# Two-layer decoder trunk on one Trainium2 core: the dilated attention stage gets a written-out order on TensorE, with scores three blocks ahead and value products of four blocks together

## The chip, the cores and the metric

The kernel runs on one core of a Trainium2 chip. The metric is device microseconds of one execution; three runs of the kernel before lie between 3378.36 and 3381.26 us. The core has five engines that work side by side, each on its own list of instructions in order: TensorE (PE in the profile, its weight loads PEld), VectorE (DVE), ScalarE (ACT), GpSimd (POOL) and SyncE (SP), which here only issues transfers. An instruction that waits holds up everything behind it on its engine, and nothing on another engine.

## The reference

Two layers; each normalises x, projects it, mixes tokens in two branches and projects back. The branch that matters here is causal attention of 12 heads of width 64 over 2048 tokens, in three patterns, whose outputs are weighted by their softmax denominators:

```python
DIL_PATTERNS = ((128, 1), (512, 4), (2048, 16))     # window, dilation
def _dilated_window(q, k, v, window, dilation):      # blocks of 128 queries of one residue class
    ...                                              # each sees its own block of keys and the one before
    s = einsum('brnqhd,brnkhd->brnhqk', qb, kk) * scale;  s = where(mask, s, -inf)
    m = max(s, -1);  p = exp(s - m);  l = sum(p, -1)
    o = einsum('brnhqk,brnkhd->brnqhd', p, vv) / l
    return o, m + log(l)
def _dilated_mixture(q, k, v):
    alpha = softmax(stack(dens, 0), 0)               # over the three patterns
    return sum(alpha[..., None] * outs, 0)
```

## The kernel before, in words

A layer is four stages: input projection, the stick-breaking branch (`_stick`), the dilated branch (`_dilated`) and the output projection. `_dilated` goes over 6 pairs of heads, for each pair over the three patterns p = 0, 1, 2, and for each pattern over 16 blocks b of 128 queries: 288 blocks in a layer. A block's work:

- **scores** on TensorE: for each of the two heads two matmuls, the high and low part of the keys (lines 758 and 759), 256 columns each;
- **minimum and mask** on VectorE, one per head (line 760), then **exp** on ScalarE (line 764). They are 128 columns wide for p = 0 and for blocks with no predecessor, and 256 otherwise;
- **transposes** of the exps on TensorE (line 772), two or four, and a copy of them out of PSUM (line 774), on VectorE or ScalarE;
- **value products** on TensorE (line 779), two or four; the trace shows each as two records. Every fourth block the sums are copied to `o3` by ScalarE (lines 785, 788, 792).

When a pair is through, `stats` turns the minima and sums into weights `wr` (some small matmuls, lines 667 to 672, and a chain of small operations), and `apply` spreads the weights by one matmul for each of 16 columns (`weighing`, line 703), multiplies `o3` by them on VectorE (line 706), and adds and gates the three patterns on POOL (lines 710 to 712). Both run during the next pair. For the last pair the weighing lies between the output projection's matmuls, in threes (lines 841, 844, 845). `make_q` reorders the queries for p = 1 and p = 2 by casts, nearly all on POOL (lines 607, 612).

**Array shapes.** The profile writes the shape in which a matmul uses the 128 x 128 array: scores, transposes and the output projection 128\*128, value products 128\*64 (64 output rows for each head), weighing 64\*128 (contraction over 64 partitions), statistics 128\*32.

**What sets the order.** A scheduler that knows the program, not the chip, orders the instructions that are not pinned. In `_stick` TensorE's instructions are pinned in the order in which they are written; in `_dilated` only the last pair's weighing and a few of the first casts are.

Of the kernel before, what the change touches and what calls it, by code (L numbers as in the profile page):

```python
# [29 lines left out]
def _constants():  # L30
# [20 lines left out]
    sel = np.zeros((64, 16, 128), f)  # L51
# [509 lines left out]
def _dilated(tc, mem, v_scr, qk_scr, g_scr, mix, masks, sel, ident, neg1):  # L561
    nc = tc.nc
    mk = mem.get("M", [128, 732])
# [8 lines left out]
    ts_s = Slices([ta[:, 0], ta[:, 1], tb[:, 0:512].rearrange("p (c h q) -> p c h q", c=2, h=2)])  # L572
# [4 lines left out]
    v_r = mem.ring("H2", "H3", "H4", "H5")  # L577
    selr = mem.get("F13", [64, NT, 128], F32R)
# [20 lines left out]
    def make_q(pr, p):  # L599
        eng = nc.vector if pr == 0 and p == 1 and 1 else nc.gpsimd  # L600
        for h in range(2):
# [3 lines left out]
            if p == 1:  # L605
                for c in range(4):
                    eng.tensor_copy(
                        tr[:, 512 * c:512 * c + 512].rearrange("p (n r a) -> p n r a", n=4, r=4),
                        qc[:, c::4].rearrange("p r (n a) -> p n r a", n=4))
            else:  # L610
                for c in range(4):
                    ins = nc.gpsimd.tensor_copy(
                        tr.rearrange("p (j c a) -> p j c a", j=NT, c=NT)[:, 4 * c:4 * c + 4],
                        qc[:, :, 32 * c:32 * c + 32].rearrange("p c (j a) -> p j c a", a=8))
                    if pr == 0:
                        tc.keep_in_program_order(ins)
# [11 lines left out]
    VAHEAD = 2  # L628
# [3 lines left out]
    for i in range(VAHEAD):  # L632
        load_v(i)

    fin = []

    def hooks(pr, p, b):
        if b % 8 == 0:
            load_v((pr * 3 + p) * 2 + b // 8 + VAHEAD)
        while fin and fin[0][0] <= 16 * p + b:  # L640
            fin.pop(0)[1]()
        if (p, b) == (0, 2):
            make_q(pr, 2)
        if pr + 1 < NPAIR:
            if (p, b) == (1, 0):
                load_k(pr + 1)
            if (p, b) == (1, 8):
                load_q(pr + 1)
            if (p, b) == (2, 4):
                make_q(pr + 1, 1)  # L650

    def stats(pr, st, wrs):
        sm = xa[0:32, 0:768].rearrange("p (s q a) -> p s q a", s=2, q=3)
        x4 = xa[:, 768:1024].rearrange("p (s n h r c) -> p s n h r c", s=2, n=4, h=2, r=4)
        x1 = gt_r.get([128, 2, 2 * NT, 8])
        nc.vector.tensor_tensor(
            out=x1, in0=st[:, :, 2].rearrange("p s h j -> p s (h j)").unsqueeze(3).to_broadcast([128, 2, 2 * NT, 8]),
            in1=mk[:, 692:700].unsqueeze(1).unsqueeze(1).to_broadcast([128, 2, 2 * NT, 8]), op=ALU.mult)
        for s in range(2):
            for h in range(2):  # L660
                nc.vector.tensor_tensor(
                    out=x4[:, s, :, h],
                    in0=st[:, s, 1, h].rearrange("p (c n) -> p n c", n=4).unsqueeze(2).to_broadcast([128, 4, 4, 4]),
                    in1=mk[:, 688:692].unsqueeze(1).unsqueeze(3).to_broadcast([128, 4, 4, 4]), op=ALU.mult)
        for s in range(2):
            ps = w_r.get([128, 512])
            nc.tensor.transpose(ps[:32, 0:128], st[:, s, 0].rearrange("p h b -> p (h b)"), ident)
            for n in range(4):
                nc.tensor.matmul(ps[:32, 128 + 32 * n:160 + 32 * n], x4[:, s, n].rearrange("p h r c -> p (h r c)"),
                                 mk[:, 700:732], start=True, stop=True)  # L670
            for h in range(2):
                nc.tensor.matmul(ps[:32, 256:384], mk[:, 656 - 16 * h:688 - 16 * h],
                                 x1[:, s, NT * h:NT * h + NT].rearrange("p j a -> p (j a)"),
                                 start=h == 0, stop=h == 1)
            nc.any.tensor_copy(sm[:, s].rearrange("p q a -> p (q a)"), ps[:32, :384])
# [19 lines left out]
    def apply(pr, o3, wrs, c4, m7=None):  # L695
# [5 lines left out]
        for c in range(4 * c4, 4 * c4 + 4):  # L701
            wb = w_r.get([128, 3, 128])
            ins = nc.tensor.matmul(wb, selr[:, c], wrs[0], start=True, stop=True)  # L703
            if final:
                tc.keep_in_program_order(ins)
# [185 lines left out]
```

## Time and profile before

| | us |
|---|---|
| median of three runs | 3379.39 |
| the profiled execution | 3379.84 |
| its span | 3378.1 |
| dilated stage, first layer (from 1027.2 to 1502.7) | 475.50 |
| of it TensorE busy | 474.81 |
| dilated stage, second layer (from 2707.5 to 3183) | 475.50 |
| of it TensorE busy | 474.56 |

The span is what the trace covers, 1.7 us less than the execution's own time. The mean granted TensorE clock is 0.998 of full speed. "Busy" runs from an instruction's start to its modelled end; TensorE's instructions overlap, so that the distance from one start to the next says more than the length of one.

### The profile page before, as it was taken

To read this page: it belongs to the slowest core of one execution; us is meant where nothing else is said; L and a number is where in the kernel's file an instruction comes from. 1 tells how busy PE (TensorE), PEld (TensorE's weight loads), DVE (VectorE), ACT (ScalarE), POOL (GpSimd) and SP (SyncE) were. 2 spreads that over 40 slices of the span, in tenths; PEclk is the share of its full clock that TensorE was granted. 3 is DMA by queue.
4 is the path that set the end of the run, shared out by engine and by line. 5 is a ranking of instruction groups with operands and counts; after the bars stand their busy time and mean duration, and the time that the engine had idled before them with its cause. 6 is when DMAs were issued, how large, how long until landed. Compare 5 with 4: busy or idle time off the path is not lost.

```text
span 3378.1 us, 67384 instructions
## 1 busy us (share of the span) xinstructions
PE 3326.0 (98%) x25808; PEld 2873.5 (85%) x25808; DVE 1735.1 (51%) x4279; ACT 1524.4 (45%) x4347; POOL 1233.6 (37%) x1200
## 2 busy tenths in 40 slices
PE   8999999999999999999999999999999999999999
PEld 8999999887777777777899999998877777777777
DVE  5034330117997777774240344301179977877721
ACT  5123321116777777761031233201167787777600
POOL 3067761104672332252021777511046722223500
PEclk9999999999999999999999999999999999999999
DMA  5122245316213555344341222452252145553443
GB/s 187 66 88 101 101 145 174 104 60 172 54 56 101 157 152 155 105 156 140 125 133 66 84 105 105 151 166 92 73 158 67 45 121 157 147 150 95 131 141 103
DMA packets 305922, 395.85 MB, mean 117 GB/s; under 512 B 16832, under 2 KB 225728, under 8 KB 295360
## 3 DMA queue, kind: packets, MB, share of 16 engines
q1 hardware_dynamic: 305600, 391.54, 37.5%
q8 instruction: 204, 3.34, 0.4%
q14 instruction: 118, 0.97, 0.1%
HBM read 234.19 MB, written 148.90 MB: 113 GB/s over the span
## 4 chain that ended last, share of the span: by engine, by line
PE 90%; DVE 3%; issue 3%; ACT 2%; POOL 2%; DMA 1%; SPq 0%; POOLq 0%; DVEq 0%; ACTq 0%
PE b L290 11%; PE b L291 11%; PE b L289 11%; PE b L779 8%; PE b L772 8%; PE b L758 5%; PE b L759 4%; PE b L841 4%; PE b L315 4%; PE b L317 3%; PE b L316 3%; PE b L844 3%; PE b L845 3%; PE b L528 3%; PE b L703 2%
## 5 line engine op out<-in xcount | busy, mean ns | idle before, releaser
L291 PE MATMUL b<-F,F 128*128 128x256 f32 x2304 | 651.8, 283 | 0.0
L764 ACT ACTIVATE H<-H,T 128x256 f32<-128x256 f32 (+1 forms) x1152 | 526.7, 460 | 126.8 <-DVE T L760 117.9
L760 DVE CUSTOM_DVE_ANT_0 H<-b,M 128x256 f32<-128x256 f32 (+1 forms) x1152 | 389.3, 362 | 144.3 <-PE b L759 85.3
L291 PEld LDWEIGHTS b<-F,F 128*128 128x128 f32 x2304 | 440.4, 191 | 0.0
L290 PE MATMUL b<-F,F 128*128 128x256 f32 x1536 | 436.3, 284 | 0.0
L289 PE MATMUL b<-F,F 128*128 128x256 f32 x1536 | 434.9, 283 | 0.0
L290 PE MATMUL b<-F,G 128*128 128x256 f32 x1536 | 434.3, 283 | 0.0
L289 PE MATMUL b<-F,G 128*128 128x256 f32 x1536 | 433.9, 283 | 0.0
L501 POOL TENSOR_TENSOR G<-G,G 128x512 f32<-128x512 f32 (+3 forms) x320 | 321.2, 1017 | 233.8 <-DVE G L495 182.1
L758 PE MATMUL b<-F,F 128*128 128x256 f32 x1152 | 378.2, 344 | 0.8 <-DVE T L760 0.6
L213 POOL TENSOR_TENSOR F<-H,F 128x1024 fp32r<-128x1024 f32 x62 | 154.8, 2512 | 608.6 <-ACT F L212 570.5
L772 PE MATMUL b<-ident,H 128*128 128x128 f32 x1800 | 353.4, 287 | 0.8 <-DVE H L774 0.2
L495 DVE TENSOR_TENSOR_SCAN G<-G,b 128x513 f32<-128x513 f32 (+3 forms) x320 | 337.1, 1087 | 24.0 <-ACT G L494 23.4
L759 PE MATMUL b<-F,F 128*128 128x256 f32 x1152 | 315.2, 287 | 0.0
L779 PE MATMUL b<-H,H 128*64 128x128 f32 x3600 | 309.9, 286 | 0.0
L289 PEld LDWEIGHTS b<-F,G 128*128 128x128 f32 x1536 | 294.9, 192 | 0.0
L289 PEld LDWEIGHTS b<-F,F 128*128 128x128 f32 x1536 | 294.7, 192 | 0.0
L290 PEld LDWEIGHTS b<-F,F 128*128 128x128 f32 x1536 | 294.7, 192 | 0.0
L290 PEld LDWEIGHTS b<-F,G 128*128 128x128 f32 x1536 | 291.9, 190 | 0.0
L772 PEld LDWEIGHTS b<-ident,H 128*128 128x128 f32 x1800 | 212.1, 141 | 75.6 <-issue 70.1
L758 PEld LDWEIGHTS b<-F,F 128*128 128x128 f32 x1152 | 227.7, 198 | 33.0 <-issue 12.4
L779 PEld LDWEIGHTS b<-H,H 128*64 128x64 f32 x3600 | 188.2, 136 | 79.1 <-issue 33.2
(152 smaller groups left out, 7061.4 us busy)
## 6 DMA issues: line engine op xcount, KB each, us to landing
qk_l<-H SPq DMA_DIRECT2D x96, 512.0 KB
F<-qk_l SPq DMA_DIRECT2D x48, 1024.0 KB
v_l<-S SPq DMA_DIRECT2D x288, 128.0 KB
H<-v_l SPq DMA_DIRECT2D x72, 512.0 KB
F<-qk_l SPq DMA_DIRECT2D x48, 512.0 KB
H<-in_w_in SPq DMA_DIRECT2D x40, 512.0 KB
g_l<-S SPq DMA_DIRECT2D x64, 256.0 KB
G<-mixa_l SPq DMA_DIRECT2D x32, 448.0 KB
```

Source lines behind the costliest of these rows:

```text
L213: (nc.vector if first else nc.gpsimd).tensor_tensor(out=wl[:, ks], in0=raw, in1=wh[:, ks].bitcast(F32), op=ALU.subtract)
L289: nc.tensor.matmul(ps, hT(q, 0, k)[:, cs], wh[:, k], start=k == 0, stop=False)
L290: nc.tensor.matmul(ps, hT(q, 0, k)[:, cs], wl[:, k], start=False, stop=False)
L291: nc.tensor.matmul(ps, hT(q, 1, k)[:, cs], wh[:, k], start=False, stop=k == NK - 1)
L495: nc.vector.tensor_tensor_scan(out=r[:, 0:n + 1][:, ::-1], data0=g[:, 512 - n:513][:, ::-1], data1=z[:, 0:1].to_broadcast([128, n + 1]), i ...
L501: nc.gpsimd.tensor_tensor(out=b[:, :n], in0=b[:, :n], in1=r[:, 1:n + 1], op=ALU.mult)
L758: nc.tensor.matmul(sc[:, h], qb, kv(kk[pr][h][0]), start=True, stop=False)
L759: nc.tensor.matmul(sc[:, h], qb, kv(kk[pr][h][1]), start=False, stop=True)
L760: nc.vector.tensor_tensor_reduce(out=pe[:, h, :un], in0=sc[:, h, u0:u0 + un], in1=mk[:, m0:m0 + un], scale=-0.125, scalar=3.0e38, op0=ALU. ...
L764: nc.scalar.activation(pe[:, h, :un], pe[:, h, :un], AF.Exp, scale=-1.0, bias=st[:, 0, p, h, b:b + 1], accum_out=st[:, 1, p, h, b:b + 1])
L772: nc.tensor.transpose(tp[:, ch, h], src, ident)
L779: nc.tensor.matmul(ob[64 * h:64 * h + 64, b % 4], vq[(pr * 3 + p) * 2 + (b - ch) // 8][:, (b - ch) % 8, 64 * h:64 * h + 64], ts[:, ch, h], ...
```

## The change

- All matmuls and transposes of `_dilated` are pinned in the order written. A step g does: scores of block g+3 (`front`), transposes and their copy of block g (`mid`), at every fourth step the value products of blocks g-4 to g-1 (`back`) and one copy of their sums, and at steps 15 to 30 of a pair one weighing matmul of the pair before (`weigh`).
- The copies of transposes alternate between VectorE and ScalarE by block. For p = 1 one copy of 512 columns to `o3` takes the place of four.
- `stats` is split: `stats_a` at step 1, `stats_b` at step 5 of the next pair, most of its elementwise work on GpSimd (VectorE for the last pair).
- The weighing matmul contracts over 128 partitions, of which the upper 64 are zero, in place of 64: `sel` and `wr` grow.
- There are five buffers for copied transposes where there were three, and three for values where there were four; values are loaded at every eighth step.

```diff
-    sel = np.zeros((64, 16, 128), f)
+    sel = np.zeros((128, 16, 128), f)
...
+    pin = tc.keep_in_program_order
-    ts_s = Slices([ta[:, 0], ta[:, 1], tb[:, 0:512].rearrange("p (c h q) -> p c h q", c=2, h=2)])
+    td = mem.get("H5", [128, 2, 2, 2, 128])
+    ts_s = Slices([td[:, 0], td[:, 1], ta[:, 0], ta[:, 1], tb[:, 0:512].rearrange("p (c h q) -> p c h q", c=2, h=2)])
-    v_r = mem.ring("H2", "H3", "H4", "H5")
-    selr = mem.get("F13", [64, NT, 128], F32R)
+    v_r = mem.ring("H2", "H3", "H4")
+    wr = mem.get("W", [128, 3, 128], F32R)
+    nc.gpsimd.memset(xz, 0.0)
+    nc.gpsimd.tensor_copy(wr[64:128], xz)
...
+    def front(g):
...
+                pin(nc.tensor.matmul(sc[:, h], qb, kv, start=s == 0, stop=s == 1))
...
+    def mid(g):
...
+                pin(nc.tensor.transpose(tp[:, ch, h], pe[:, h, 128 * w:128 * w + 128], ident))
+        ts = ts_s.get()
+        (nc.vector.tensor_copy if g % 2 else nc.scalar.copy)(ts[:, :nch], tp[:, :nch])
...
+    def back(g0):
...
+        for b in range(b0, b0 + 4):
+            ts = tss.pop(g0 + b - b0)
+            nch = 1 if geom(p, b)[2] else 2
+            for ch in range(nch):
+                for h in range(2):
+                    pin(nc.tensor.matmul(
+                        ob[64 * h:64 * h + 64, b % 4],
...
-        nc.vector.tensor_tensor(out=ew, in0=ew, in1=mn.unsqueeze(1).to_broadcast([32, 3, 128]), op=ALU.mult)
-        wr = mem.get("W", [64, 3, 128], F32R)
-        nc.vector.tensor_copy(wr[0:32], ew)
-        nc.vector.tensor_tensor(out=ew, in0=ew, in1=wr[0:32].bitcast(F32), op=ALU.subtract)
-        nc.vector.tensor_copy(wr[32:64], ew)
+        eng.tensor_tensor(out=ew, in0=ew, in1=mn.unsqueeze(1).to_broadcast([32, 3, 128]), op=ALU.mult)
+        eng.tensor_copy(wr[0:32], ew)
+        eng.tensor_tensor(out=ew, in0=ew, in1=wr[0:32].bitcast(F32), op=ALU.subtract)
+        eng.tensor_copy(wr[32:64], ew)
...
+    def weigh(pr, c):
...
+        pin(nc.tensor.matmul(wb, selr[:, c], wr, start=True, stop=True))
+        nc.vector.tensor_tensor(out=o3[:, :, c], in0=o3[:, :, c], in1=wb, op=ALU.mult)
...
+    LEAD = 3
+    total = NPAIR * 48
+    for g in range(LEAD):
+        front(g)
+    for g in range(total):
+        pr, t = g // 48, g % 48
+        if t % 8 == 2:
+            load_v(g // 8 + 1)
+        if t == 2:
+            make_q(pr, 2)
+        if pr + 1 < NPAIR:
+            if t == 16:
+                load_k(pr + 1)
+            if t == 24:
+                load_q(pr + 1)
+            if t == 36:
+                make_q(pr + 1, 1)
+        if g + LEAD < total:
+            front(g + LEAD)
+        mid(g)
+        if g % 4 == 0 and g:
+            back(g - 4)
+        if pr:
+            if t == 1:
+                stats_a(pr - 1, nc.gpsimd)
+            elif t == 5:
+                stats_b(pr - 1, nc.gpsimd)
+            elif 15 <= t < 31:
+                weigh(pr - 1, t - 15)
+                if t % 4 == 2:
+                    gate(pr - 1, (t - 15) // 4)
+        yield
+    back(total - 4)
```

On TensorE, in the middle of p = 2 of a pair, the order before is this (b_ names are PSUM tiles, F_ keys and queries, H_ exps, copied transposes and values):

```order
L758 MATMUL b_1295_12621<-F_1071_11032,F_1186_11822 128x256
L759 MATMUL b_1295_12621<-F_1072_11033,F_1186_11822 128x256
L779 MATMUL b_1278_12478<-H_895_9808,H_1220_12051 64x128 x4
L772 MATMUL b_1290_12572<-ident,H_893_9806 128x128 x4
L758 MATMUL b_1293_12601<-F_1073_11037,F_1187_11827 128x256
L759 MATMUL b_1293_12601<-F_1074_11038,F_1187_11827 128x256
L758 MATMUL b_1298_12641<-F_1071_11032,F_1186_11822 128x256
L759 MATMUL b_1298_12641<-F_1072_11033,F_1186_11822 128x256
L772 MATMUL b_1292_12591<-ident,H_894_9807 128x128 x4
L758 MATMUL b_1295_12621<-F_1073_11037,F_1187_11827 128x256
L759 MATMUL b_1295_12621<-F_1074_11038,F_1187_11827 128x256
L779 MATMUL b_1288_12558<-H_895_9808,H_1243_12217 64x128 x2
```

In the changed kernel the same place reads as follows (line 676 is the scores, 697 the transposes, 711 the value products):

```order
L676 MATMUL b_1423_13434<-F_1204_11990,F_1315_12739 128x256
L676 MATMUL b_1423_13434<-F_1205_11991,F_1315_12739 128x256
L676 MATMUL b_1423_13434<-F_1206_11995,F_1316_12744 128x256
L676 MATMUL b_1423_13434<-F_1207_11996,F_1316_12744 128x256
L697 MATMUL b_1424_13443<-ident,H_894_9807 128x128 x4
L676 MATMUL b_1427_13459<-F_1204_11990,F_1315_12739 128x256
L676 MATMUL b_1427_13459<-F_1205_11991,F_1315_12739 128x256
L676 MATMUL b_1427_13459<-F_1206_11995,F_1316_12744 128x256
L676 MATMUL b_1427_13459<-F_1207_11996,F_1316_12744 128x256
L697 MATMUL b_1428_13468<-ident,H_893_9806 128x128 x4
L711 MATMUL b_1429_13474<-H_895_9808,H_1395_13242 64x128 x2
L711 MATMUL b_1429_13474<-H_896_9809,H_1395_13242 64x128 x4
L711 MATMUL b_1429_13474<-H_897_9810,H_1395_13242 64x128 x8
```

Scores now come in fours, and the value products of four blocks in one piece of 14 or 16. Runs of value products in a layer go from 251 to 72, and places where the array shape differs from that of the matmul ahead from 663 to 150, both counted over the whole of TensorE's order.

On GpSimd, before, the casts of `make_q` for p = 2 (line 612) stand among the gate's additions (G_ is `o3`):

```order
L607 CAST F_1274_12453<-F_1244_12219 128x512 x4
L607 CAST F_1275_12458<-F_1245_12221 128x512 x4
L612 CAST F_1336_12843<-F_1244_12219 128x512 x4
L710 TENSOR_TENSOR G_1154_11678<-G_1154_11678 128x512
L612 CAST F_1337_12848<-F_1245_12221 128x512 x4
```

In the changed kernel the second head's casts (now line 616) stand ahead of the last four operations that make the weights `wr` (W):

```order
L616 CAST F_1316_12744<-F_1238_12182 128x512 x4
L767 TENSOR_TENSOR H_896_9809<-H_896_9809 32x384
L768 CAST W_9812<-H_896_9809 32x384
L769 TENSOR_TENSOR H_896_9809<-H_896_9809,W_9812 32x384
L770 CAST W_9812<-H_896_9809 32x384
L789 TENSOR_TENSOR G_1151_11632<-G_1151_11632 128x512
```

The weights are now made on GpSimd behind these casts, whose target buffer is that of the first queries of the pair, free only after the scores of block 15.

## Rows read from the trace of the kernel before

**Rows 1.** Windows: start:end, length, busy of PE, PEld, DVE, ACT, POOL; clock, DMA share.
```profile
830.00:1000.00 170.00, 160.00 (x1494) 129.23 (x1493) 158.95 (x189) 132.47 (x295) 113.84 (x115) 0.99 0.18 54
1027.20:1502.70 475.50, 474.81 (x4133) 366.56 (x4131) 370.50 (x1511) 373.86 (x1435) 147.38 (x171) 1.00 0.47 138
```

**Rows 2.** TensorE groups by form, dilated stage: busy, mean ns | idle before.
```profile
L772 PE MATMUL b<-ident,H 128*128 128x128 f32 x900 | 176.7, 287 | 0.3
...
L672 PE MATMUL b<-S,M 128*32 128x128 f32 x48 | 6.4, 276 | 0.0
```

**Rows 3.** Timeline of TensorE, p = 2: start, length, operation.
```profile
1243.01 0.49 PE L772 MATMUL b<-ident,H 128*128 128x128 f32 x3
1243.43 0.66 PE L779 MATMUL b<-H,H 128*64 128x128 f32 x8
...
1252.91 0.37 PE L758 MATMUL b<-F,F 128*128 128x256 f32 x1
...
1253.51 0.61 PE L772 MATMUL b<-ident,H 128*128 128x128 f32 x4
1253.88 0.36 PE L758 MATMUL b<-F,F 128*128 128x256 f32 x1
...
1254.31 1.09 PE L779 MATMUL b<-H,H 128*64 128x128 f32 x16
1255.33 0.33 PE L772 MATMUL b<-ident,H 128*128 128x128 f32 x1
```

**Rows 4.** Timeline of TensorE, p = 1.
```profile
1147.58 0.36 PE L758 MATMUL b<-F,F 128*128 128x256 f32 x1
...
1148.13 0.27 PE L772 MATMUL b<-ident,H 128*128 128x128 f32 x1
```

**Rows 5.** Timeline of TensorE, a weighing inside the stage.
```profile
1195.68 0.61 PE L703 MATMUL b<-W,F 64*128 64x384 f32 x2
1196.23 0.44 PE L779 MATMUL b<-H,H 128*64 128x128 f32 x4
1196.60 0.33 PE L772 MATMUL b<-ident,H 128*128 128x128 f32 x1
```

**Rows 6.** Timeline of TensorE, last weighing between output matmuls.
```profile
1514.12 0.44 PE L703 MATMUL b<-W,F 64*128 64x384 f32 x1
1514.49 0.50 PE L841 MATMUL b<-F,H 128*128 128x512 f32 x1
...
1515.38 0.44 PE L703 MATMUL b<-W,F 64*128 64x384 f32 x1
```

**Rows 7.** Timeline of TensorE, the last value products of the stick stage.
```profile
1033.55 0.44 PE L528 MATMUL b<-G,F 128*64 128x128 f32 x4
```

**Rows 8.** Timeline of ScalarE, p = 0.
```profile
1111.14 0.40 ACT L764 ACTIVATE H<-H,T 128x128 f32<-128x128 f32 x1
...
1111.53 0.36 ACT L774 COPY H<-b 128x256 f32<-128x256 f32 x1
1111.78 0.41 ACT L764 ACTIVATE H<-H,T 128x128 f32<-128x128 f32 x1
```

**Rows 9.** Groups by form, dilated stage, the other engines.
```profile
L764 ACT ACTIVATE H<-H,T 128x256 f32<-128x256 f32 x324 | 163.8, 507 | 50.2 <-DVE T L760 46.7
...
L760 DVE CUSTOM_DVE_ANT_0 H<-b,M 128x256 f32<-128x256 f32 x324 | 129.1, 420 | 41.4 <-PE b L759 28.6 <-PE b L772 5.4 <-ACT H L764 4.2
...
L774 DVE COPY H<-b 128x512 f32<-128x512 f32 x138 | 94.8, 687 | 13.2 <-PE b L772 12.5 <-PE b L779 0.6
...
L706 DVE TENSOR_TENSOR G<-G,b 128x384 f32<-128x384 f32 x80 | 43.8, 553 | 11.7 <-PE b L703 11.1
...
L612 POOL CAST F<-F 128x512 fp32r<-128x512 f32 x48 | 29.8, 663 | 19.5 <-issue 15.1 <-PE b L759 4.4
...
L710 POOL TENSOR_TENSOR G<-G 128x512 f32<-128x512 f32 x20 | 25.5, 1276 | 110.1 <-DVE G L706 94.0 <-PE b L772 16.1
...
L785 ACT COPY G<-b 128x512 f32<-128x512 f32 x24 | 14.0, 582 | 5.7 <-PE b L779 5.2
```

More of the change, by code (lines that the diff above doesn't have):

```diff
@@ L599, in make_q @@
     def make_q(pr, p):
-        eng = nc.vector if pr == 0 and p == 1 and 1 else nc.gpsimd
+        eng = nc.vector if pr == 0 and p == 1 else nc.gpsimd
         for h in range(2):
@@ L604, in make_q @@
             tr = t.bitcast(F32R)
-            if p == 1:
-                for c in range(4):
+            for c in range(4):
+                if p == 1:
                     eng.tensor_copy(
@@ L652, in stats, with geom @@
-    def stats(pr, st, wrs):
-        sm = xa[0:32, 0:768].rearrange("p (s q a) -> p s q a", s=2, q=3)
+    load_v(0)
+    yield
+    selr = mem.get("F13", [128, NT, 128], F32R)
+    for i in range(4):
+        t = gt_r.get([128, 4, 128])
+        nc.sync.dma_start(out=t, in_=sel[:, 4 * i:4 * i + 4])
+        nc.gpsimd.tensor_copy(selr[:, 4 * i:4 * i + 4], t)
+    o3s, sts = {}, {}
+    def geom(p, b):
+        if p == 0:
+            return b, 0, True
+        c, n = (b // 4, b % 4) if p == 1 else (0, b)
+        return c, n, n == 0
@@ new lines, in _dilated @@
+    pes, tss = {}, {}
+    def mid(g):
+        p, b = g // 16 % 3, g % 16
+        first = geom(p, b)[2]
+        pe = pes.pop(g)
+        tp = t_r.get([128, 2, 2, 128])
+        nch = 1 if first else 2
+        for ch in range(nch):
+            for h in range(2):
+                w = 0 if first else 1 - ch
+                pin(nc.tensor.transpose(tp[:, ch, h], pe[:, h, 128 * w:128 * w + 128], ident))
+        ts = ts_s.get()
+        (nc.vector.tensor_copy if g % 2 else nc.scalar.copy)(ts[:, :nch], tp[:, :nch])
+        tss[g] = ts
@@ L696, in apply, with gate @@
+    def gate(pr, c4, m7=None):
         final = pr == NPAIR - 1
         cs = slice(4 * c4, 4 * c4 + 4)
-        gt = gt_r.get([128, 4, 128])
-        nc.sync.dma_start(out=gt, in_=g_scr[2 + pr, :, 512 * c4:512 * c4 + 512].rearrange(
-            "p (c a) -> p c a", c=4))
[L701 to L705, printed above, removed]
-            nc.vector.tensor_tensor(out=o3[:, :, c], in0=o3[:, :, c], in1=wb, op=ALU.mult)
-            if final:
-                yield
+        o3, gt = o3s[pr], gts[pr]
@@ L801, in _dilated @@
+    back(total - 4)
     m7 = [mem.get("F5", [128, NT, 128], F32R), mem.get("F6", [128, NT, 128], F32R)]
-    stats(NPAIR - 1, st, wrs)
+    stats_a(NPAIR - 1, nc.vector)
+    stats_b(NPAIR - 1, nc.vector)
     yield m7
     for c4 in range(4):
-        yield from apply(NPAIR - 1, o3, wrs, c4, m7)
+        for c in range(4 * c4, 4 * c4 + 4):
+            weigh(NPAIR - 1, c)
+            yield
+        gate(NPAIR - 1, c4, m7)
 def _output(tc, mem, layer, mix, m7, w_out, x_src, x_dst, proj):
```

198 lines of the change are left out of this document (80 added, 118 removed).

## The prediction, made before the changed kernel ran

> **What bounds the kernel now.** I read the windows first. In the first layer's dilated stage TensorE is busy for 474.81 of 475.50 us at a granted clock of 1.00, while VectorE has 370.50, ScalarE 373.86 and GpSimd 147.38 [rows 1]. The groups agree: the transposes, which depend on VectorE and ScalarE, found TensorE idle for 0.3 us in all [rows 2]. So the stage is worth what TensorE's order is worth, and nothing that only removes waits helps. The timeline then shows what TensorE is busy with: starts, not lengths, give the price of a piece, and it depends on the piece behind it. Four transposes ahead of scores take 0.37 (1253.51 to 1253.88). Three ahead of value products take 0.42 (1243.01 to 1243.43) [rows 3], where their own share of the 0.37 would be 0.26 to 0.28: changing from the 128\*128 shape to 128\*64 costs some 0.16. Value products: a run of four takes 0.37 [rows 5], a run of sixteen 1.02 [rows 3], so 0.054 for one record more and 0.15 for the run as such. One weighing matmul between 128\*128 work takes 0.37 [rows 6], two 0.55 [rows 5]: 0.18 for the second. The time to be had is in these edges.
>
> **What the change does to TensorE.** No matmul goes away; they are regrouped. Prices of pieces after the change, from starts:
>
> - four scores and then transposes: 0.55 for p = 0 and 1 [rows 4], 0.60 for p = 2 (1252.91 to 1253.51, [rows 3]); four transposes and then scores 0.37 [rows 3]; two by estimate 0.14 to 0.18, of which I take 0.14.
> - p = 0 of a pair: 16 x (0.55 + 0.14) = 11.0. p = 1: 12 x (0.55 + 0.37) + 4 x 0.69 = 13.8. p = 2: 15 x 0.97 + 0.74 = 15.3. Together 40.1.
> - value products: runs of 16, 28 or 32 records: 1.02, 1.02 + 12 x 0.054 = 1.68, 1.90. A pair has 4 x 1.02 + 5 x 1.68 + 3 x 1.90 = 18.2, and 12 x 0.2 for the edges in and out (0.16 in, and some 0.04 for scores that follow) = 2.4.
> - six pairs: 6 x 60.7 = 364. Weighing without a change of shape, 80 x 0.18 = 14.4: the 64 zero rows add contraction, no columns. Statistics, five sets at 1.5 (busy 6.4 / 6 = 1.07 for the larger products of a set [rows 2], the rest by estimate) = 7.5.
>
> TensorE's own work is then 386 us a layer, 89 less. Counted the other way: 251 - 72 = 179 runs of value products at about 0.36 for both edges and the start is 64, weighing 80 x (0.37 - 0.18) is up to 15, and score runs of two that become fours the rest.
>
> There is a lower floor too: weight loads are busy for only 366.56 of the 475.50 us [rows 1]. The Trainium skill, "Perfetto Trace Analysis", Identifying the Most-Contended Engine, calls matmul busy time a bad measure of headroom and the share of weight loads the good one. That 474.81 us "busy" hold so much idle array agrees with it; by it the stage could come to 367.
>
> **What it adds.** With TensorE at 386, the other engines come close, and now the order is fixed: what is late is waited for.
>
> - *ScalarE in p = 0.* Four blocks need eight exps 0.39 apart, two copies at 0.25 [rows 8] and a copy to `o3` of 0.58 [rows 9]: 4.20 us. TensorE needs 4 x 0.69 + 1.02 + 0.2 = 3.98. Over four such groups that is 0.9 a pair, and 0.6 for the statistics' copies and exp that stand in ScalarE's queue behind VectorE and GpSimd: 1.5 x 6 = 9.
> - *Weights behind casts.* The order shows GpSimd's four casts of the second head ahead of the weights. They wait for the scores of block 15, then 4 x 0.66, then (by the lengths of rows 9, scaled to 384 columns) 2 x 0.96 + 2 x 0.50, 5.6 us in all. Between those scores and the first weighing TensorE has three pairs of scores, four of transposes and one run of value products, 3 x 0.55 + 4 x 0.14 + 1.2 = 3.4. A wait of 0 to 2.2; I take 1.5, as ScalarE delays TensorE there too: 5 x 1.5 = 7.5. Everything on TensorE is queued behind that weighing.
> - *VectorE while weighing.* It falls into p = 1. Four blocks have on VectorE six minima at 0.42, two at about 0.29, two copies at 0.69, four multiplications at 0.55 [rows 9]: 6.7 by busy time. TensorE has 13.8 / 4 + 1.68 + 0.2 + 4 x 0.18 = 6.05. The best that VectorE shows in a pinned stage is 158.95 busy in 170 us (the stick stage, [rows 1]); by that the four take 7.1, 1.1 more than TensorE, but busy times overlap at their ends, which may make it none. Half: about 0.7 x 4 x 5 = 14.
>
> Waits: 30.5 a layer (0 to about 61 as bounds). ScalarE's whole load is a check: 373.86, plus some 30 to 36 more copies of blocks at 0.58, less what the single copies for p = 1 save, is about 391; at the 93.5% share that VectorE reached in the stick stage it needs 418, against my 386 + 30.5 = 416.5.
>
> - *Start.* Before, the first scores slip in at 1027.2, ahead of the stick stage's last value products, which start at 1033.55 [rows 7]. Pinned behind them, and without the scores that lay between, the stage starts at about 1032.5, and filling three blocks of lead takes 1.
> - *End.* Weighing and three output matmuls repeat every 1.26 us [rows 6]; without the two changes of shape 0.18 + 0.70 = 0.88. Sixteen times 0.38 is 6.1; about 1.5 of it I give to the statistics, all now in line: 4.6.
> - *Transfers.* Three value buffers in place of four. A load for the next eight blocks is issued some ten steps before its use, behind up to 2.5 MB of queries, gates and values. 138 GB/s at a DMA share of 0.47 [rows 1] is 294 GB/s when full, so 8.5 us or six to seven steps: hidden, at no cost. If the gate's stores hold up the queue by three steps more, some 3 us a pair show.
>
> Stage end: 1032.5 + 1 + 386 + 30.5 = 1450.0 in place of 1502.7: 52.7, and 4.6 behind it: 57.3 a layer. The second layer's stage is the same. Two layers are 114.6; the profiled execution took 3379.84 (0.45 above the median), so **3265 us**.
>
> **The rivals.**
>
> - *No waits.* Five buffers and three blocks of lead carry every burst: 30.5 more a layer, 3204. For it: VectorE and ScalarE have less than 400 each on average. Against: the two queues are in order and serve each other, and the sums above put them ahead of TensorE in places.
> - *Waits twice as large.* VectorE, ScalarE and GpSimd each hold up the other: 3326. For it: the tie in p = 0 and the weights' chain; against: ScalarE's check gives no more than 418.
> - *Slower: the loop is longer than the lead.* From the end of a block's scores to its transposes: minima and exps, the second half of each overlapped, about 1.2 (0.42 + 0.51 and half of the rest, [rows 9]); queued between them can be two copies, a copy to `o3` and a multiplication, 0.69 + 0.58 + 0.58 + 0.55 = 2.4, and a neighbour's minima and exps, 0.84 + 0.98. That is 3.6 to 5.4, where TensorE has three steps of p = 2 without value products, 3 x 0.97 = 2.9. One window in four has none, so the wait comes once in four blocks, 72 times a layer. The gain is gone when it is (52.7 + 30.5 + 4.6) / 72 = 1.2 us each time. At half way between 0.7 and 2.5, 1.6 to 1.7, the stage takes 122 more than 386, and the time is 3448. For it: nothing else on TensorE can step in any more. Against: VectorE and ScalarE have no such backlog all the time; their sums give about 0.4 a window.
> - *Weight loads alone are the floor.* Were every edge to go, waits too, the stage would take 367 and the time 3379.84 - 2 x (475.5 - 366.6) = 3162. Against: the pieces of rows 3 to 5 keep their own distances.
> - *It doesn't do what it says.* The edges are not prices of the shape but short waits for copies that the profile counts as busy. Then regrouping gives back little, 3372 or so. For it: edges often stand where data change hands. Against: the last sixteen weighings [rows 6] all use the same weights, long there, and pay the same 0.37. The Trainium skill, "TensorEngine Tiling (Array Packing)", Key Properties, says that changing the tiling mode drains TensorE; it gives no price, and it speaks against this rival.
>
> **Chances.** Forecast, 3235 to 3295: 0.47. No waits, about 3204: 0.16. Weight loads alone, 3162: 0.02. Twice the waits, about 3326: 0.24. Slower: 0.06. Little change: 0.05. The range that leaves no more than 2 in 10 outside is 3195 to 3340. A measurement tells 0.2% from no change, 6.8 us. Faster 0.91, the same 0.03, slower 0.06.
>
> **What would show it.** Right: the dilated stage is 410 to 425 us; value products come 72 times in runs of 16 to 32, at 1.0 to 1.9 us; a weighing takes about 0.18 between scores; TensorE idles some 30 us, mostly ahead of transposes and of the first weighing, released by ScalarE and by GpSimd's last cast. Wrong: transposes idle for over 100 us in all (the loop), scores or value products still at the old distances without idle time (the edges are something else), or value products that wait for a transfer.

## The result and the profile after

The changed kernel took 3268.98 us (median of four runs, 3266.42 to 3269.61), the kernel before 3380.27 in the same measurement: a ratio of 0.967, interval 0.9653 to 0.9687. The forecast was 3265, in a range of 3195 to 3340. The profiled executions are 3379.84 and 3269.15 us: 110.7 gained, 55.3 a layer. The sum came out nearly; three of its terms did not, and they offset each other.

Windows of the changed kernel (start:end, length, busy of PE, PEld, DVE, ACT, POOL; clock, DMA share, GB/s): its first dilated stage, the 38.9 us behind it, and a pair's p = 1 with its weighings:

```profile
1035.40:1441.10 405.70, 395.76 (x4090) 362.89 (x4088) 298.80 (x1399) 366.10 (x1388) 175.41 (x222) 1.00 0.55 157
1441.10:1480.00 38.90, 31.15 (x113) 22.55 (x113) 27.56 (x35) 12.12 (x20) 22.72 (x19) 0.82 0.51 162
1119.10:1142.10 23.00, 23.00 (x233) 21.80 (x233) 21.49 (x84) 20.73 (x75) 13.59 (x16) 1.00 0.45 144
```

The stage is 405.70 us where it was 475.50 [rows 1], and still TensorE's: 395.76 busy at a clock of 1.00. VectorE fell to 298.80. Weight loads fill 362.89 / 405.70 = 89% in place of 77%. TensorE's groups by form in that stage (the last number is the idle time before them, with its releasers):

```profile
L676 PE MATMUL b<-F,F 128*128 128x256 f32 x1152 | 205.8, 303 | 0.1
L697 PE MATMUL b<-ident,H 128*128 128x128 f32 x900 | 146.3, 273 | 5.5 <-ACT H L699 3.2 <-DVE H L699 1.6 <-ACT H L682 0.6
L711 PE MATMUL b<-H,H 128*64 128x128 f32 x1800 | 114.5, 277 | 0.4 <-DVE H L699 0.4
L781 PE MATMUL b<-W,F 128*128 128x384 f32 x80 | 34.3, 429 | 3.9 <-POOL W L770 3.9
```

Idle is 9.9 us in all: 5.5 ahead of transposes, where [rows 2] had 0.3, and 3.9 ahead of weighings, released by GpSimd's last cast. None of TensorE's idle time in the stage is released by a transfer. Two stretches of TensorE's timeline show the new pieces (start, length, operation), the first with weighings, in p = 1, the second from the last steps of p = 2, where the scores are already those of the next pair's p = 0:

```profile
1120.13 0.44 PE L781 MATMUL b<-W,F 128*128 128x384 f32 x1
1120.41 0.63 PE L676 MATMUL b<-F,F 128*128 128x256 f32 x4
1120.88 0.60 PE L697 MATMUL b<-ident,H 128*128 128x128 f32 x4
1121.24 0.42 PE L781 MATMUL b<-W,F 128*128 128x384 f32 x1
1121.50 0.64 PE L676 MATMUL b<-F,F 128*128 128x256 f32 x4
...
1124.46 1.75 PE L711 MATMUL b<-H,H 128*64 128x128 f32 x28
1126.14 0.44 PE L781 MATMUL b<-W,F 128*128 128x384 f32 x1
```

```profile
1097.50 0.60 PE L697 MATMUL b<-ident,H 128*128 128x128 f32 x4
1097.85 0.73 PE L676 MATMUL b<-F,F 128*128 128x256 f32 x4
1098.41 0.38 PE L697 MATMUL b<-ident,H 128*128 128x128 f32 x2
1098.72 1.97 PE L711 MATMUL b<-H,H 128*64 128x128 f32 x32
1100.62 0.74 PE L676 MATMUL b<-F,F 128*128 128x256 f32 x4
```

The prices that the forecast took from rows 3 to 6 are there: four transposes and then scores 0.35 (1097.50 to 1097.85), four scores and then transposes 0.56 here and 0.61 within p = 2 (1085.10 to 1085.71), 32 records of value products 1.90 (1098.72 to 1100.62; the edge in is in the 0.31 ahead of them), 28 records 1.68. A weighing between transposes and scores takes 0.26, and the scores behind it 0.47 in place of 0.56: 0.18 net.

Two things lie outside the stage. First, its start, the changed kernel's last stick matmuls and first scores:

```profile
1033.43 0.87 PE L528 MATMUL b<-G,F 128*64 128x128 f32 x10 [0.51 <-DVE G L516]
...
1034.60 0.89 PE L528 MATMUL b<-G,F 128*64 128x128 f32 x12
1035.42 2.55 PE L676 MATMUL b<-F,F 128*128 128x256 f32 x16
```

Scores begin at 1035.42, 8.1 us later than before (1027.27), behind the stick stage's last value products. Of these, 1.0 us had come earlier: the stick stage's first value product starts at 805.99 in place of 804.94, behind stages whose code is the same in both kernels. Second, what follows the stage:

```profile
1441.13 0.50 PE L876 MATMUL b<-F,H 128*128 128x512 f32 x1
...
1443.80 0.40 PE L880 MATMUL b<-F,H 128*128 128x512 f32 x1
1446.09 0.67 PE L876 MATMUL b<-F,H 128*128 128x512 f32 x1 [1.90 <-ACT F L860]
1447.43 0.79 PE L879 MATMUL b<-F,H 128*128 128x512 f32 x1 [0.68 <-POOL F L861]
...
1452.24 0.79 PE L876 MATMUL b<-F,H 128*128 128x512 f32 x1 [1.74 <-ACT F L860]
1455.14 0.79 PE L879 MATMUL b<-F,H 128*128 128x512 f32 x1 [2.11 <-POOL F L861]
1455.73 0.63 PE L880 MATMUL b<-F,H 128*128 128x512 f32 x1
1456.16 0.63 PE L876 MATMUL b<-F,H 128*128 128x512 f32 x1
...
1459.97 0.40 PE L876 MATMUL b<-F,H 128*128 128x512 f32 x1
1460.20 0.40 PE L879 MATMUL b<-F,H 128*128 128x512 f32 x1
...
1461.37 0.34 PE L781 MATMUL b<-W,F 128*128 128x384 f32 x1
...
1462.26 0.34 PE L781 MATMUL b<-W,F 128*128 128x384 f32 x1
```

The output projection starts at 1441.13, 61.6 us earlier than before, and then waits for its weights: 1.90, 0.68, 1.74, 2.11 us, for ScalarE's casts (line 860) and GpSimd's differences (line 861). In between its matmuls are 0.43 apart in place of 0.23, at half the clock. The first weighing among them comes 20.2 us after the first output matmul; before, 10.2. Weighings are then 0.89 apart, against 1.26 in [rows 6]. The same stretch of the kernel before had no such waits:

```profile
1502.70:1541.60 38.90, 38.15 (x147) 24.89 (x147) 28.03 (x39) 9.40 (x14) 19.04 (x16) 1.00 0.44 142
```

SyncE's queue shows that what the casts read is asked for late. In the changed kernel the first four loads of output weights are issued 23.5 us ahead of the first output matmul, behind stores of the fifth pair's gated sums:

```profile
1410.25 7.30 SPq L796 DMA_DIRECT2D mixa_l<-S  x2
1417.65 1.81 SPq L859 DMA_DIRECT2D G<-in_w_out  x4
```

In the kernel before it was 37 us (1465.74 to 1502.69):

```profile
1465.74 1.81 SPq L824 DMA_DIRECT2D G<-in_w_out  x4
```

Those loads go into the buffer that held the fifth pair's sums (`G0`), and its weighing now ends at step 30 of the last pair.

### The profile page after: what moved, and what is told of

Read it like the earlier page. It is cut to its first block, busy times and chain, and to the rows that moved or that the text cites. A ratio compares the mean times of both kernels' runs of the same rounds, so it can differ in the third digit from the quotient of the medians.

```text
span 3267.4 us, 66732 instructions
## 1 busy us (share of the span) xinstructions
PE 3177.5 (97%) x25808; PEld 2880.8 (88%) x25808; DVE 1605.1 (49%) x4067; ACT 1521.4 (47%) x4277; POOL 1317.2 (40%) x1342
## 4 chain that ended last, share of the span: by engine, by line
PE 82%; DVE 5%; ACT 4%; POOL 4%; issue 3%; DMA 2%; SPq 0%; POOLq 0%; DVEq 0%; ACTq 0%
PE b L290 11%; PE b L291 11%; PE b L289 11%; PE b L676 7%; PE b L711 5%; PE b L697 5%; PE b L315 4%; PE b L317 4%; PE b L316 4%; PE b L879 3%; PE b L880 3%; PE b L876 3%; PE b L528 2%; PE b L393 2%; DVE G L495 2%
## 5 line engine op out<-in xcount | busy, mean ns | idle before, releaser
L291 PE MATMUL b<-F,F 128*128 128x256 f32 x2304 | 651.8, 283 | 0.0
L678 DVE CUSTOM_DVE_ANT_0 H<-b,M 128x256 f32<-128x256 f32 (+1 forms) x1152 | 368.2, 360 | 168.8 <-PE b L676 62.7
L291 PEld LDWEIGHTS b<-F,F 128*128 128x128 f32 x2304 | 440.4, 191 | 0.0
L290 PE MATMUL b<-F,F 128*128 128x256 f32 x1536 | 436.3, 284 | 0.0
L289 PE MATMUL b<-F,F 128*128 128x256 f32 x1536 | 434.9, 283 | 0.0
L676 PE MATMUL b<-F,F 128*128 128x256 f32 x2304 | 412.0, 303 | 0.3
L676 PEld LDWEIGHTS b<-F,F 128*128 128x128 f32 x2304 | 326.3, 190 | 20.1 <-issue 19.5
L697 PE MATMUL b<-ident,H 128*128 128x128 f32 x1800 | 293.0, 274 | 11.0 <-ACT H L699 5.5
L289 PEld LDWEIGHTS b<-F,F 128*128 128x128 f32 x1536 | 294.7, 192 | 0.0
L290 PEld LDWEIGHTS b<-F,F 128*128 128x128 f32 x1536 | 294.7, 192 | 0.0
L711 PE MATMUL b<-H,H 128*64 128x128 f32 x3600 | 229.5, 277 | 0.8 <-DVE H L699 0.8
L493 ACT ACTIVATE G<-b 128x512 f32<-128x512 f32 (+3 forms) x320 | 180.4, 566 | 103.5 <-PE b L486 88.3
L337 DVE COPY S<-b 128x512 f32<-128x512 f32 x48 | 33.2, 691 | 390.5 <-PE b L291 347.9
```

The lines of the kernel that those rows point to most:

```text
L289: nc.tensor.matmul(ps, hT(q, 0, k)[:, cs], wh[:, k], start=k == 0, stop=False)
L290: nc.tensor.matmul(ps, hT(q, 0, k)[:, cs], wl[:, k], start=False, stop=False)
L291: nc.tensor.matmul(ps, hT(q, 1, k)[:, cs], wh[:, k], start=False, stop=k == NK - 1)
L493: nc.scalar.activation(g[:, 512 - n:512], z[:, :n], AF.Sigmoid, scale=-0.125)
L676: pin(nc.tensor.matmul(sc[:, h], qb, kv, start=s == 0, stop=s == 1))
L678: nc.vector.tensor_tensor_reduce(out=pe[:, h, :un], in0=sc[:, h, u0:u0 + un], in1=mk[:, m0:m0 + un], scale=-0.125, scalar=3.0e38, op0=ALU. ...
```

## The experiments

Each experiment is one edit against the changed kernel (e4: against the kernel before). Stage: from the first score to the first output matmul, first and second layer. Wait: from the first output matmul to the first weighing among them, likewise.

The kernel before took 3379.98 to 3382.03 us (medians) in the measurements of e1 to e12, so differences of one or two us between kernels of different measurements say nothing.

| kernel | median us | against the changed kernel | stage | wait |
|---|---|---|---|---|
| before | 3380.27 | +111.3 | 475.4, 475.9 | 10.2, 9.9 |
| changed | 3268.98 | | 405.7, 408.5 | 20.2, 19.4 |
| e1_k64 | 3328.10 | +59.1 | 431.8, 431.6 | 19.7, 18.8 |
| e2_v2 | 3304.64 | +35.7 | 428.0, 425.7 | 20.7, 15.7 |
| e3_v1 | 3414.42 | +145.4 | 483.6, 483.2 | 16.8, 14.3 |
| e4_before_w128 | 3331.63 | +62.7 | 456.9, 456.0 | 10.6, 9.9 |
| e5_tail | 3258.66 | -10.3 | 413.0, 415.2 | 8.5, 8.5 |
| e6_start | 3261.15 | -7.8 | 409.3, 408.1 | 19.9, 20.0 |
| e7_p0_vector | 3263.70 | -5.3 | 405.1, 403.8 | 19.8, 18.3 |
| e8_lead2 | 3293.02 | +24.0 | 424.4, 423.0 | 15.6, 12.6 |
| e9_weights_vector | 3265.27 | -3.7 | 406.2, 407.3 | 19.6, 19.5 |
| e10_no_pins | 3352.91 | +83.9 | 446.0, 445.6 | 7.1, 7.4 |
| e11_mended | 3251.48 | -17.5 | 413.7, 413.5 | 8.5, 8.5 |
| e12_mended_weights | 3258.54 | -10.4 | 413.0, 422.6 | 8.5, 8.5 |

Of e5 to e12, only e11 and e12 have an interval of the ratio to the kernel before that lies clear of the changed kernel's (0.9653 to 0.9687). Those of e5 (to 0.9656), e6 (to 0.966) and e7 (to 0.9667) overlap with it a little, though all their runs are below all of the changed kernel's.

**Theory: an edge between array shapes has a price. Rival: edges are short waits for data.** Five kernels. e1, the weighing over 64 partitions again:

```diff
-        pin(nc.tensor.matmul(wb, selr[:, c], wr, start=True, stop=True))
+        pin(nc.tensor.matmul(wb, selr[0:64, c], wr[0:64], start=True, stop=True))
```

> The changed kernel with one edit undone: the weighing matmul contracts over 64 partitions again (shape 64*128), everything else as changed. Shape theory: a weighing between 128*128 work costs 0.37 us again in place of 0.18, 80 times in a stage, so 15 us a layer, and 16 x 0.38 = 6 us a layer between the output matmuls: about 42 us more than the changed kernel, some 3311 us. Rival (the edges were short waits for data, not the price of a shape): the order is the same, so the time stays near 3269 us.

The ratio to the kernel before is 0.9845 (0.983 to 0.986). The order is the same and so is the data, and only the shape differs; the rival falls for the weighing. The stage took 26 us more, not 15. Its timeline at the place of the rows above:

```profile
1120.54 0.60 PE L697 MATMUL b<-ident,H 128*128 128x128 f32 x4
1121.07 0.44 PE L781 MATMUL b<-W,F 64*128 64x384 f32 x1
1121.43 0.75 PE L676 MATMUL b<-F,F 128*128 128x256 f32 x4
1122.02 0.60 PE L697 MATMUL b<-ident,H 128*128 128x128 f32 x4
```

Transposes ahead of the weighing 0.53 in place of 0.36, the weighing 0.36 in place of 0.26, the scores behind it 0.59 in place of 0.47: 0.39 for a weighing between transposes and scores, as 55 of the 80 are by the trace (0.38 at the median). The other 25, 20 of them directly behind value products, where the shape changes anyway, cost about 0.20 each: together 26, as measured. The estimate had looked at one piece alone; an edge is paid in the pieces on both sides.

Value products of two blocks (e2) at every second step; for e3, of one block, it is `if g: back1(g - 1)` at every step. `back1` is `back` for one block, with the copy of the sums after every fourth:

```diff
-        if g % 4 == 0 and g:
-            back(g - 4)
+        if g % 2 == 0 and g:
+            back1(g - 2)
+            back1(g - 1)
```

> The changed kernel with value products of two blocks together instead of four; 144 runs a layer instead of 72. Shape theory: 72 more runs at about 0.36 us each (edges and start) are 26 us a layer, 52 in all, some 3321 us. Rival (edges are waits): smaller pieces that come earlier leave the time near 3269 us or a little under.

> The changed kernel with the value products of each block on their own, one step behind its transposes; 288 runs a layer instead of 72. Shape theory: 216 x 0.36 = 78 us a layer, about 3425 us, so that the pinned order alone is slower than the kernel before, which had 251 runs. Rival (it is the pinning and the lead of three that gained): under 3300 us.

e3 gives 77.9 us more in the first stage for 216 more runs, 0.36 each, and is slower than the kernel before (1.0102, 1.0087 to 1.0117): a pinned order with a lead of three, without the grouping, loses, even with the padded weighing. e2 gives 22.3 and 17.2 for 72 more runs, 0.31 and 0.24 each. These differences hold waits too. In e3 most of TensorE's idle time stands ahead of the value products:

```profile
L718 PE MATMUL b<-H,H 128*64 128x128 f32 x1800 | 161.9, 289 | 14.4 <-ACT G L731 8.9 <-ACT G L726 2.1 <-ACT H L699 1.4
```

TensorE's idle time in the two stages is 9.9 and 11.3 us in the changed kernel, 5.9 and 5.4 in e2, 14.6 and 14.3 in e3; and in the changed kernel's second stage and e2's first the clock was at half for 3.41 us, some 1.7 us of work by estimate. With both taken out, a run costs about 0.34 in all four comparisons. The rival falls for the value products too: 0.36 was nearly right, and e3's 0.36 holds some waiting. That this price is one of the shape, as for the weighing, and not of the run as such, e2 and e3 don't show.

e4, the padded weighing alone, in the kernel before:

```diff
-    sel = np.zeros((64, 16, 128), f)
+    sel = np.zeros((128, 16, 128), f)
...
-    selr = mem.get("F13", [64, NT, 128], F32R)
+    selr = mem.get("F13", [128, NT, 128], F32R)
+    wr = mem.get("W", [128, 3, 128], F32R)
...
+    nc.gpsimd.memset(xz, 0.0)
+    nc.gpsimd.tensor_copy(wr[64:128], xz)
...
```

> The kernel before with one part of the change alone: selection and weights on 128 partitions, the upper 64 zero, so that the weighing matmul has the 128*128 shape. Shape theory: 16 x 0.38 = 6 us a layer among the output matmuls, and up to 15 us a layer in the stage, less where a weighing stood next to value products: 20 to 40 us under the kernel before, 3340 to 3360 us. Rival (twice the rows cost something, or the edges are waits): no change, near 3380 us.

48.3 us under the kernel before (0.9856, 0.984 to 0.9873), 18.5 and 19.9 in the stages. One edit of a few lines is over two fifths of the whole gain, more than forecast for the same reason as in e1. The order of TensorE's 4130 instructions in the first stage is that of the kernel before. A weighing between transposes and four scores (15 of them) takes with these two neighbours 0.88 in place of 1.41, and one between two runs of value products (10) 1.1 as before: the gain is there only where the padding took a change of shape away.

e10, no pins:

```diff
-    pin = tc.keep_in_program_order
+    pin = lambda ins: ins
```

> The changed kernel without the pins in the dilated stage: the scheduler orders TensorE again. Counted in its order, value products stand in 192 runs a layer, where the changed kernel has 72 and the kernel before 252; scores and transposes in 250 and 254 runs. Shape theory: 120 x 0.36 = 43 us a layer more, less some 10 of waits that a free order avoids, 3330 to 3350 us. Rival (writing the products of four blocks together is enough): 3270 us or less.

The stages took 40.3 and 37.1 us more; 43 was worked out for the runs alone, and the time lies just above the 3330 to 3350 expected. Writing the products of four blocks together does not keep them together: the pins do. How much of the 40 is theirs and how much that of the scores and transposes, which move too, isn't shown.

The rest of the change (statistics on GpSimd, copies divided between two engines, more buffers) was not taken back piece by piece; what each part of it is worth isn't known.

**Theory: the tail waits for a buffer that comes free late.** In the last pair:

```diff
-            if t == 1:
-                stats_a(pr - 1, nc.gpsimd)
+            final = pr == NPAIR - 1
+            if t == 1:
+                stats_a(pr - 1, nc.vector if final else nc.gpsimd)
...
+            elif final and 11 <= t < 19:
+                weigh(pr - 1, 2 * (t - 11))
+                weigh(pr - 1, 2 * (t - 11) + 1)
+                if t % 2 == 0:
+                    gate(pr - 1, (t - 11) // 2)
-            elif 15 <= t < 31:
+            elif not final and 15 <= t < 31:
```

> The changed kernel, with the fifth pair's weighing and gating earlier in the last pair: its statistics elementwise on VectorE, and two weighing matmuls a step at steps 11 to 18 in place of one at steps 15 to 30. The output stage's loads go into the buffer that holds this pair's sums. Theory (after the change the output stage waits, because that buffer is given up only when the gating is done): loads start some 10 us earlier, the 20 us from the first output matmul to the first weighing among them fall to 10 to 12, and the time to about 3250 us. Rival (the casts of the output weights or the transfers themselves are what is late): the same wait, and the time stays near 3269 us or rises, since VectorE now gets two multiplications a step.

The first four loads are issued at 1411.56, 36.3 us ahead of the first output matmul, nearly as in the kernel before. The wait fell to 8.5 us in both layers, and the clock of the same 38.9 us went back to 1.00:

```profile
1447.80:1486.70 38.90, 38.27 (x171) 30.83 (x171) 33.56 (x44) 10.39 (x17) 20.65 (x17) 1.00 0.52 160
```

So the late end of the fifth pair's weighing and gating is the cause, and the rival (casts or transfers slow in themselves) falls: the output projection, from its first matmul's start to its last's, took 185.7 and 182.2 us in place of 198.2 and 193.1. Whether the loads are held by the buffer itself or by the stores of the gated sums ahead of them in SyncE's queue isn't separated, since e5 moves both. But the stage grew by 7.3 and 6.7 us, and only 10.3 of 22.6 came out. In the last pair's p = 0, which took 26.9 us where the changed kernel's took 19.7, TensorE stood at the first weighing, since step 11 was too early for the weights, and the clock behind that wait was at half:

```profile
1386.19 1.01 PE L781 MATMUL b<-W,F 128*128 128x384 f32 x2 [3.69 <-DVE W L770]
```

```profile
1386.20:1392.40 6.20, 6.20 (x33) 5.54 (x33) 2.62 (x9) 1.74 (x6) 2.48 (x5) 0.50 0.01 3
```

By estimate half the clock costs 3.1 us beyond the wait there. Part of the 7.2 us is only moved, with the weighings, from p = 1.

**Smaller terms.** e6, scores of the first blocks inside the stick stage's last steps:

```diff
-            if i == 50:
+            if i in (50, 77, 78, 79):
                 next(dl)
...
     for g in range(LEAD):
         front(g)
+        yield
...
```

The edit also moves the load of the selection matrix behind these scores, and takes a pair's buffer for the sums at its first value products.

> The changed kernel, with the scores of the first three blocks written into the last three steps of the stick stage. Theory (pinned behind the stick stage, the first scores start 8 us later than before, while TensorE waits there for other engines): first scores some 5 to 8 us earlier, some 4 us a layer gained, about 3261 us. Rival (what follows is bound by the stick stage's last transposes and the first blocks' own chain): under 1 us a layer, 3267 to 3269 us.

The first layer's scores start 5.1 us earlier (1030.3); from the stick stage's first value product it is 4.8 us, and 4.7 in the second layer. The median is 7.8 us lower (runs of 3258.76 to 3264.33), as the theory had it. In the profiled execution, 4.8 us shorter, it is uneven: the last output matmul of the first layer starts 0.4 us earlier, that of the second 4.8, since the first layer's stage is 3.6 us longer, 2.7 of it in the first pair's p = 0. So in the first layer the early start is given back nearly whole, in the second it is kept, and why is open.

e7, no copies of transposes on ScalarE in p = 0:

```diff
-        (nc.vector.tensor_copy if g % 2 else nc.scalar.copy)(ts[:, :nch], tp[:, :nch])
+        (nc.vector.tensor_copy if g % 2 or p == 0 else nc.scalar.copy)(ts[:, :nch], tp[:, :nch])
```

> The changed kernel, with all copies of transposes for p = 0 on VectorE, none on ScalarE. Theory (ScalarE is over-full in p = 0: 4.2 us for four blocks against TensorE's 4.0): the waits in p = 0 outside the first weighing, some 4 us a layer, go, and the time is about 3262 us. Rival (those waits are latency of a chain that crosses three engines): no change, 3267 to 3270 us.

5.3 us (runs of 3261.93 to 3265.09), 0.6 and 4.7 of it in the two stages. ScalarE in p = 0 costs something, less than the 5.4 a layer (0.9 a pair) of the forecast; the uneven halves don't settle how much. Of the 4.7, some 1.7 is by estimate the fall of the clock in the changed kernel's second stage, which e7 doesn't have. In both layers the first pair's p = 0 went from 16.2 to 14.8 us; the p = 0 of the other five pairs together got no shorter.

e8, a lead of two:

```diff
-    LEAD = 3
+    LEAD = 2
```

> The changed kernel with scores two blocks ahead in place of three. Theory of the loop (a block needs 2.5 us or so from its scores to its transposes, and two steps give 1.4 to 1.9): waits at most steps, 30 us a layer or more, 3330 us or above. Rival (only the engines' sums count, the lead has slack): near 3269 us.

The stages took 18.7 and 14.6 us more, about half of what was expected, and not at most steps: in the first stage 17.5 of it lies in the last transposes ahead of value products, 71 places, on average 0.51 for two in place of 0.32 and 0.96 for four in place of 0.54. That is once in four blocks, where the forecast's slow rival looked for it. About half of it the profile counts as busy. The lead does carry the loop, though the loop is shorter than that rival had it.

e9, the last steps of the weights on VectorE:

```diff
...
-        eng.tensor_copy(wr[0:32], ew)
-        eng.tensor_tensor(out=ew, in0=ew, in1=wr[0:32].bitcast(F32), op=ALU.subtract)
-        eng.tensor_copy(wr[32:64], ew)
+        nc.vector.tensor_copy(wr[0:32], ew)
+        nc.vector.tensor_tensor(out=ew, in0=ew, in1=wr[0:32].bitcast(F32), op=ALU.subtract)
+        nc.vector.tensor_copy(wr[32:64], ew)
```

> The changed kernel, with the last four operations that make the weights on VectorE in place of GpSimd, so that they do not stand behind the casts of the next queries. Theory (the first weighing of a pair waits for casts that wait for block 15): the wait ahead of it, some 3 to 5 us a layer, goes, about 3261 us. Rival (VectorE's own queue makes the weights as late): no change, 3266 to 3271 us.

The multiplication ahead of them goes to VectorE as well. Inconclusive: runs from 3263.66 to 3270.94 overlap with the changed kernel's, and the stages are no shorter (406.2, 407.3). That the wait exists is seen on GpSimd in the changed kernel, in the third pair:

```profile
1180.35 2.28 POOL L616 CAST F<-F 128x512 fp32r<-128x512 f32 x4 [0.89 <-PE b L676]
1182.59 1.00 POOL L767 TENSOR_TENSOR H<-H 32x384 f32<-32x384 f32 x1
1183.65 0.49 POOL L768 CAST W<-H 32x384 fp32r<-32x384 f32 x1
1184.23 0.99 POOL L769 TENSOR_TENSOR H<-H,W 32x384 f32<-32x384 f32 x1
1185.29 0.49 POOL L770 CAST W<-H 32x384 fp32r<-32x384 f32 x1
```

and on TensorE:

```profile
1185.83 0.45 PE L781 MATMUL b<-W,F 128*128 128x384 f32 x1 [1.68 <-POOL W L770]
```

The casts wait for block 15's scores and take 2.28, the four operations behind them 3.2, and TensorE starts the weighing when the last is through. But the third and the last pair gained 1.5 to 1.9 us in p = 1 in e9, and the fourth lost 3.4 there: its first weighing waited 1.72 us for VectorE's last cast of the weights (until 1255.30), and the granted clock of the 4.7 us behind it was 0.64. VectorE's order makes its own lateness.

**Together.** e11 has e5 (with steps 14 to 21), e6 and e7; e12 adds e9.

> The changed kernel with three mends: the fifth pair's weighing two a step at steps 14 to 21 of the last pair with its statistics on VectorE, the first three blocks' scores inside the stick stage's last steps, and the copies of transposes for p = 0 on VectorE. Theory (the gains of the three add, and the wait of e5 for weights that were not ready at step 11 goes): 12 us a layer at the output, 4 at the start, 3 in p = 0, about 3233 us. Rival (what one mend wins another stage takes back): 3245 to 3255 us.

> As e11, and with the last four operations that make the weights on VectorE for all pairs. Theory: another 3 to 5 us a layer, about 3226 us. Rival (VectorE, which has all copies of p = 0 here, is the one that is late): the time of e11 or above it.

e11 is the fastest of all: 0.9614 of the kernel before (0.9601 to 0.9628), clear of the changed kernel's interval. But it is 17.5 us under the changed kernel, where its parts were to give 36: its rival was right. The waits at the output are gone (8.5 us), yet the last pair takes 80.9 us in place of 76.7, 28.0 of them in p = 1 against 24.5: TensorE idles for 2.2 us at the first weighing there, released by VectorE's last cast of the weights, and the clock is at half for 3.41 us behind it (from 1390.07). That the rest comes from two multiplications a step on VectorE, and from casts of output weights that now stand in ScalarE's and GpSimd's queues while blocks are still to be done, is argued, not shown. In e12 the weights on VectorE lose 7 us; its second stage is 9.1 us longer than e11's. In that stage the weighings wait:

```profile
L776 PE MATMUL b<-W,F 128*128 128x384 f32 x80 | 34.3, 438 | 12.7 <-DVE W L765 12.5
```

In its first stage they wait for 2.4 us in all. In the second, the first weighing of the second to the fifth pair waits for 2.58 each, and behind three of these waits the clock was at half for 3.41 us, as in 2733.10 to 2736.40. Why VectorE makes the weights later in the second layer is open.

## Why the prediction was right, and which of its terms were not

- **TensorE as the bound, and prices of pieces from starts: right.** With every piece of the first stage at the lower quartile of its kind, and 2.4 for the scores ahead of the first transposes, TensorE's own work is 390 us, against 386 and 1 for the filling; by how finely the kinds are divided it comes to 388 to 393. Value products take 1.02, 1.68 and 1.90 as forecast, a weighing 0.18, two transposes 0.14; statistics 2.0 a set in place of 1.5. e1 and e4, where little but the shape of the weighing differs, show that edges between shapes have a price, and e2, e3 and e10 that a run of value products has one. "It doesn't do what it says" is out.
- **Waits: mis-sized, 15.6 us in place of 30.5.** (405.7 less 390.1; 13 to 17 by the other divisions. 9.9 of it shows as idle time.) By place, about: the first weighing of a pair 5.2 (7.5), the rest of p = 0 5.3 (9), p = 1 with the weighings 1.4 (14), p = 2 3.7 (none). The step that failed is "*VectorE while weighing*": its 6.7 us for four blocks were a sum of mean lengths from rows 9. In the window 1119.10 to 1142.10 VectorE is busy 21.49 of 23.00 us, 5.4 for four blocks, since neighbouring instructions overlap; TensorE is busy for all 23.00 us. VectorE at 93% did not hold up TensorE there at all. The forecast's own step slipped as well: half of its 1.1 us is 0.55, which makes 11, not 14. Its check was off too: ScalarE's whole load was put at 391 us and came to 366.10.
- **Start: 7.1 us late in place of 5.3** (8.1 less the 1.0 from the stages ahead), and 5.7 in the second layer. With all scores gone from it, the stick stage's end still waits for VectorE (0.51 us ahead of 1033.43). e6 shows that nearly 5 us a layer of it can be had at this place; of it 0.4 us is left at the end of the first layer and 4.8 at the end of the second.
- **End: the wrong sign.** "About 1.5 of it I give to the statistics": the weighings among the output matmuls did gain, 25.9 to 22.1 us in the first layer and 21.3 in the second. But the output projection as a whole, from the start of its first matmul to that of its last, went from 192.2 to 198.2 and from 188.5 to 193.1 us: 6.0 and 4.6 lost where 4.6 were to be gained. The forecast followed the stage to its last matmul and did not ask what the faster stage runs into: weights whose loads come only behind a step that the change ties to step 30 of the last pair. e5 shows it.
- **The sum.** First layer, against forecast: stage 405.7 in place of 417.5 with its filling (+11.8), start -2.8 (1.0 of it from the stages ahead), end -10.6: 57.3 - 1.6 = 55.7, as measured (55.3 a layer). The total was right because two errors of some 11 us met, which is luck; the stage itself, at 405.7, lies under the 410 to 425 that the forecast gave as its sign of being right. In the second layer the stage is 408.5, with 1.4 us more idle time and the clock at half for 3.41 us.
- **The rivals.** The loop did not outgrow the lead of three; e8 shows that at two it does, by 15 to 19 us a layer. The loads of values cost nothing, as forecast: none of TensorE's idle time in the stage was released by one. Weight loads are at 89%, and 367 us were not reached, since edges and waits remain. The Trainium skill, "Perfetto Trace Analysis", Identifying the Most-Contended Engine, judges TensorE's headroom by that share, beside the share of peak arithmetic (MFU); the trace agrees as to the direction, 77% and then 89% where "busy" read 99.9% and 97.5%.

## What to carry to other kernels

When TensorE is busy all the time, price its pieces by the distance from start to start and look for pieces that change shape: group them, pin the group, or pad the small contraction with zeros, which alone gave 48 us here, and nothing where both neighbours had another shape anyway. Charge an edge to both neighbours. When a stage gets shorter, go on reading past its end: list what the next stage needs and which step gives up the buffer for it.

## What the hardware showed unasked

The granted clock behind a wait. After the wait of 1.90 us at the start of the output projection, the changed kernel's matmuls are 0.43 apart in place of 0.23, with more waits among them (0.68, 1.74, 2.11); this window has a granted clock of 0.50, the lower level of 1.2 GHz:

```profile
1447.40:1459.50 12.10, 8.01 (x16) 5.09 (x17) 7.67 (x8) 3.17 (x6) 7.33 (x6) 0.50 0.68 229
```

From 1459.97 on it is back at 2.4 GHz. The clock also fell inside a stage: in e2, behind a single wait of 1.94 us, four scores took 0.81 (1121.00 to 1121.81) in place of 0.58 (1124.70 to 1125.28):

```profile
1120.63 0.44 PE L718 MATMUL b<-H,H 128*64 128x128 f32 x4 [1.94 <-DVE H L699]
1121.00 1.00 PE L676 MATMUL b<-F,F 128*128 128x256 f32 x4
1121.81 0.63 PE L697 MATMUL b<-ident,H 128*128 128x128 f32 x2
...
1124.70 0.74 PE L676 MATMUL b<-F,F 128*128 128x256 f32 x4
1125.28 0.38 PE L697 MATMUL b<-ident,H 128*128 128x128 f32 x2
```

The granted clock of that window:

```profile
1120.60:1123.60 3.00, 2.96 (x16) 2.51 (x16) 1.41 (x10) 2.23 (x9) 2.77 (x4) 0.62 0.49 137
```

A wait of two microseconds cost more than itself there, and e5, without the waits at the output, kept the clock at 1.00 in that stretch. Not every such wait does it: behind the changed kernel's waits of 1.68 and 1.67 us for the weights in the first layer the clock stayed at 1.00 (1185.80 to 1190.00, 1388.20 to 1392.00), and behind one of 1.70 in the second it was 0.50 (3016.40 to 3019.80). What decides is not shown.
